# A hybrid encoder layer on one core: the turn of the weights' places in SBUF moved on by one at the end of the first block

## The chip, the core and the metric

The kernel runs on one core of one Trainium2 chip. The metric is the device time of one execution in microseconds (us). Runs of the kernel before took 1068.94 us in the median of three (1068.38 to 1069.08). A profile shows one execution with its five engines: TensorE (PE, with its weight loads as PEld), VectorE (DVE), ScalarE (ACT), GpSimd (POOL) and SyncE (SP, which here only issues transfers).

## The reference

One encoder layer works on 512 tokens of 1024 channels in float32. In the reference's own words, cut to what matters:

```python
x = x + 0.5 * g1 * swiglu(h, w_ffn1_in, w_ffn1_out)          # first feed-forward
h = modulate(rmsnorm(x, norm_mix), sh2, sc2)
qa, ka, va, qb, kb, vb, ga, gb = jnp.split(h @ w_in, SPLIT_POINTS, axis=-1)
ya = window_gqa_sink(rope(qa), rope(ka), va, sink_a) @ w_branch_a
ob = diff_attention(rope(qb), rope(kb), vb, lam)
yb = rmsnorm(ob, subln_b) * (1 - lam_init) @ w_branch_b
x = x + g2 * ((sigmoid(ga) * ya + sigmoid(gb) * yb) @ w_out)  # the mixers
x = x + 0.5 * g3 * swiglu(h3, w_ffn2_in, w_ffn2_out)          # second feed-forward
```

The shifts, scales and gates `sh`, `sc`, `g` come from a product of the conditioning vector with a large matrix `w_mod`. `swiglu` is a product to gate and up halves, `silu(gate) * up`, and a product back. The hidden width is 2816. `ga` and `gb`, 1024 columns each, are the gates of the two mixers: 16 chunks of 128 columns.

## The kernel before

**Three products for one.** Each float32 matrix product is made of three products of numbers in a shorter format. An operand is split in a high part (its value cast) and a low part (what the cast left out), and `mm3` issues high·high, high·low and low·high. So each block of weights is loaded into a `raw` buffer (a ring of four) and split in two: ACT casts the high part, and DVE subtracts to get the low part (`split_from`, L185). For the gates and some projections `load_main` (L1006 to L1014) makes the low part another way: ACT writes the negated high part (L1012), and a transfer issued by POOL adds the weights to it in memory from HBM (L1013).

**The places.** The high parts of all these blocks lie in one tile `high`, the low parts in one tile `low`. Both have five places (`HILO`) of 1024 columns and, at the end, 16 spare columns (`ASIDE`). `high_low` (L192) gives the places out in turn; a counter `turn` modulo five says which is next, and places that a holder still keeps are passed over. A user may lie some columns aside in its place, by `aside` (16 for many; 64 or 56 with blocks of 768 columns in Out1). A block of 1024 columns that lies 16 aside in place i ends 16 columns inside place i+1. In place 4 alone it ends in the spare columns. Whoever shares columns with an earlier user waits for that user's last read, whether he is in the same place or in the one beside it.

**Stages.** The first feed-forward runs in chunks of the hidden width; for each, `Out1` (class at L781) multiplies back. Its last instance (`final`) takes the eight output chunks m in order: m 0 to 3 lie 64 aside, m 4 lies 56 aside, m 5 to 7 lie 16 aside (L802). Then come the boundary to the mixers, `w_vb`, the projections, and the two attentions. In the attention stretch the 16 gate chunks are filler for PE: `gates` (L1106) loads each with `load_main`; gates 3 and 4 are made early, gate 5 (`EARLY_A`) is 16 aside like the projections ahead of it (`project_pairs`, L1083), and gates 6 to 15 are not aside. The branch products `w_yb` and `w_ya` follow. In the second half of `w_ya` the four units lie (16, 16, 0, 0) aside. The output mix has (0, 0, 0, 0, 0, 0, 16, 16), and all of the second feed-forward lies 16 aside.

**What sets the order.** A planner in the kernel writes the main steps and, beside them, small steps with due times. A scheduler then orders the instructions of each engine by what it knows of their dependences, and that includes the columns shared in `high` and `low`. On the chip each engine takes its instructions in that order, and waits at the first that is not ready. The attention steps are scores (L182), exponentials on ACT (L1237), sums and scalings on DVE (L1246 to L1248), transposes on PE (L1150) with a split behind them (L185), products with the values, and a norm with one step on POOL (L1308 to L1314).

The lines of the changed kernel behind L805 have numbers higher by three.

Of the kernel before, what the change touches and what calls it, by code (L numbers as in the profile page):

```python
# [97 lines left out]
RAW, HILO, F2 = 4, 5, 8  # L98
# [36 lines left out]
def layer(ctx: ExitStack, tc: tile.TileContext, a: dict):  # L135
# [48 lines left out]
    def split_from(hi, lo, src):  # L184
        last = S.copy(hi, src), V.tensor_tensor(lo, src, f(hi), ALU.subtract)  # L185
        split[:] = [i.ins for i in last]
# [3 lines left out]
    turn, holders = [0], {}  # L190

    def high_low(n=1024, aside=0, holder=None):  # L192
        while turn[0] % HILO in holders:
            turn[0] += 1
        i = turn[0] % HILO
        turn[0] += 1
        if holder:
            holders[i] = holder
        i = i * 1024 + aside
        return tuple(t[:, i : i + n] for t in parts)  # L200
# [241 lines left out]
    class Unit:  # L442
# [33 lines left out]
        def prepare(self, q):  # L476

            if q in self.ready:
                return
            self.ask(q)  # L480
            n = self.depth * 2 * P
            if q in self.apart:
                both = b8().rearrange("p a b -> p (a b)")
                hi, lo = both[:, 0:n], both[:, 1024 : 1024 + n]
            else:
                hi, lo = high_low(n, ASIDE, (self, q))
            t = self.at[q]
            with tc.issue_after(copied[0]) if q in self.in_order and copied else nullcontext():
                split_from(hi, lo, t)
            self.ready[q] = hi, lo  # L490
            if q in self.more:
                s, src = self.more[q]
                G.dma_start(t, self.srcs[src], accum_op=ALU.add)
                self.at[s] = t
# [286 lines left out]
    class Out1:  # L781
# [17 lines left out]
        def prepare(self, m):  # L799
            if m not in self.ready:  # L800
                self.ask(m)
                aside = FAR if not self.by_halves(m) else STEP_1 if m == NC - LAST_1 else ASIDE  # L802
                t = self.ready[m] = high_low(self.depth * P, aside, (self, m))
                with tc.issue_after(copied[0]):
                    split_from(*t, self.at[m])  # L805
# [1159 lines left out]
```

## Time and profile before

| what | before |
|---|---|
| median of three runs | 1068.94 us (1068.38 to 1069.08) |
| profiled execution, whole | 1068.76 us |
| its span | 1067.0 us |
| mean granted clock of TensorE | 0.995 |
| PE busy | 1047.6 us (98%) |
| DVE busy | 792.1 us (74%) |
| ACT busy | 569.3 us (53%) |
| POOL busy | 154.0 us (14%) |
| moved to and from HBM | 220.53 MB, mean 207 GB/s |

A row of waits names an engine and line, what it waited for, the total in us, how often, and the longest. A row of a timeline names the start, the duration, engine, line, operation, the tile written and the tiles read, their sizes, how many instructions the row joins, and in brackets the idle time before it and what ended it. Matmuls overlap: a row's duration is longer than the distance to the next start. A windows row gives the window, its length, the busy time of each engine with its instructions, the granted clock, the busy share of the transfer engines and GB/s. The chain of work goes back from the last instruction to what released it at each step.

### The profile page before, as it was taken

The page shows a single profiled execution, that of the slowest core. Times are in us where ns is not written, and L with a number is a line of the kernel's source. Part 1 is how long each engine was busy: PE and PEld are TensorE (multiplying, and loading weights), DVE is VectorE, ACT ScalarE, POOL GpSimd, SP SyncE. Part 2 cuts the span into 40 slices and gives each one's busy share as a digit, 9 for nine tenths or more (in the row PEclk, how much of TensorE's full clock was granted, in tenths as well). Part 3 has the DMA queues.
Part 4 walks back from the last instruction along what each step waited for, and adds up shares of the span by engine and source line. Part 5 has one row for each costly group of instructions (what it writes and reads, how often), then busy time and mean ns, then how long its engine had stood idle before and what let it go on. Part 6 is the DMA issues. An engine that isn't in the chain of part 4 may idle for free.

```text
span 1067.0 us, 18682 instructions
## 1 busy us (share of the span) xinstructions
PE 1047.6 (98%) x7330; PEld 957.1 (90%) x7330; DVE 792.1 (74%) x1449; ACT 569.3 (53%) x937; POOL 154.0 (14%) x173
## 2 busy tenths in 40 slices
PE   8999999999999999999899999999999999999998
PEld 5789899899998988899678788989999999999997
DVE  6877667567795779858664577976888787877867
ACT  5645334234354433666666755534766646654553
POOL 1010010100110100452311101001111211112210
PEclk9999999999999999999899999999999999999999
DMA  9888786966885369793647843974498998989974
GB/s 351 306 245 205 212 226 186 271 173 176 251 202 173 119 246 409 216 248 91 168 93 188 226 150 100 364 236 113 102 220 185 221 233 216 221 223 219 207 149 124
DMA packets 69081, 220.53 MB, mean 207 GB/s; under 512 B 8320, under 2 KB 11008, under 8 KB 68992
## 3 DMA queue, kind: packets, MB, share of 16 engines
q1 hardware_dynamic: 46512, 146.52, 38.5%
q0 software_dynamic: 19344, 68.30, 34.4%
q10 hardware_dynamic: 3136, 4.51, 1.2%
q8 instruction: 57, 0.93, 0.3%
q14 instruction: 32, 0.26, 0.1%
HBM read 209.07 MB, written 10.23 MB: 206 GB/s over the span
## 4 chain that ended last, share of the span: by engine, by line
PE 75%; issue 9%; DMA 5%; DVE 5%; ACT 4%; POOL 2%; ACTq 0%; POOLq 0%; DVEq 0%; SPq 0%
PE sc L174 5%; PE sc L176 5%; PE sc L175 5%; PE sc L438 5%; PE sc L440 5%; PE sc L439 4%; PE acc L176 4%; PE acc L174 4%; PE acc L175 4%; PE acc L438 4%; PE acc L440 4%; PE acc L439 4%; PE acc L1072 2%; PE acc L1074 2%; PE acc L1073 2%
## 5 line engine op out<-in xcount | busy, mean ns | idle before, releaser
L185 ACT CAST high<-raw 128x1024 fp32r<-128x1024 f32 (+2 forms) x162 | 158.1, 985 | 158.8 <-PE acc L439 37.3
L185 DVE TENSOR_TENSOR low<-raw,high 128x1024 fp32r<-128x1024 f32 (+2 forms) x162 | 183.7, 1141 | 48.7 <-ACT high L185 47.6
L438 PE MATMUL acc<-b,high 128*128 128x256 f32 x508 | 141.6, 279 | 0.1
L439 PE MATMUL acc<-b,high 128*128 128x256 f32 x508 | 141.3, 278 | 0.1
L440 PE MATMUL acc<-b,low 128*128 128x256 f32 x508 | 141.3, 278 | 0.0
L438 PE MATMUL sc<-b,high 128*128 128x256 f32 x500 | 138.7, 277 | 1.3 <-ACT f L515 1.3
L440 PE MATMUL sc<-b,low 128*128 128x256 f32 x500 | 138.8, 278 | 0.9 <-DVE low L185 0.9
L439 PE MATMUL sc<-b,high 128*128 128x256 f32 x500 | 138.5, 277 | 0.0
L185 DVE TENSOR_TENSOR low<-u,high 128x1024 fp32r<-128x1024 f32 (+1 forms) x73 | 87.5, 1200 | 32.0 <-ACT high L185 30.7
L185 ACT CAST high<-u 128x1024 fp32r<-128x1024 f32 (+1 forms) x73 | 75.5, 1036 | 57.5 <-PE sc L175 15.6
L174 PE MATMUL sc<-b,high 128*128 128x512 f32 (+1 forms) x280 | 100.6, 359 | 0.0
L175 PE MATMUL sc<-b,high 128*128 128x512 f32 (+1 forms) x280 | 100.3, 358 | 0.0
L176 PE MATMUL sc<-b,low 128*128 128x512 f32 (+1 forms) x280 | 100.3, 358 | 0.0
L438 PEld LDWEIGHTS acc<-b,high 128*128 128x128 f32 x508 | 96.0, 189 | 0.6 <-DVE f L517 0.3
L439 PEld LDWEIGHTS acc<-b,high 128*128 128x128 f32 x508 | 96.1, 189 | 0.4 <-DVE b L1754 0.3
L440 PEld LDWEIGHTS acc<-b,low 128*128 128x128 f32 x508 | 96.0, 189 | 0.2 <-DVE low L185 0.2
L438 PEld LDWEIGHTS sc<-b,high 128*128 128x128 f32 x500 | 94.1, 188 | 1.7 <-ACT f L515 1.7
L440 PEld LDWEIGHTS sc<-b,low 128*128 128x128 f32 x500 | 93.9, 188 | 1.4 <-DVE low L185 1.3
L176 PE MATMUL acc<-b,low 128*128 128x512 f32 (+1 forms) x248 | 91.2, 368 | 3.6 <-DMA low<-w_gate 3.6
L439 PEld LDWEIGHTS sc<-b,high 128*128 128x128 f32 x500 | 94.0, 188 | 0.0
L174 PE MATMUL acc<-b,high 128*128 128x512 f32 (+1 forms) x248 | 93.1, 376 | 0.0
L175 PE MATMUL acc<-b,high 128*128 128x512 f32 (+1 forms) x248 | 90.9, 367 | 0.0
(371 smaller groups left out, 2676.6 us busy)
## 6 DMA issues: line engine op xcount, KB each, us to landing
u<-w_mod SPq DMA_DIRECT2D x40, 512.0 KB, 8.4
b<-w_mod SPq DMA_DIRECT2D x32, 512.0 KB, 5.9
raw<-w2i SPq DMA_DIRECT2D x31, 512.0 KB, 5.4
u<-w2i POOLq DMA_DIRECT2D x31, 512.0 KB, 7.3
u<-w1u POOLq DMA_DIRECT2D x24, 512.0 KB, 7.8
raw<-w1u SPq DMA_DIRECT2D x24, 512.0 KB, 6.9
raw<-w1o SPq DMA_DIRECT2D x24, 384.0 KB, 3.9
raw<-w_gate SPq DMA_DIRECT2D x16, 512.0 KB, 5.2
```

The costliest lines, as they stand in the source:

```text
L174: PE.matmul(out, wh, xh, start=first, stop=False)
L175: PE.matmul(out, wh, xl, start=False, stop=False)
L176: PE.matmul(out, wl, xh, start=False, stop=last)
L185: last = S.copy(hi, src), V.tensor_tensor(lo, src, f(hi), ALU.subtract)
L438: PE.matmul(out, wh[:, s], xh, start=first and j == 0, stop=False, skip_group_check=True)
L439: PE.matmul(out, wh[:, s], xl, start=False, stop=False, skip_group_check=True)
L440: PE.matmul(out, wl[:, s], xh, start=False, stop=last and j == 1, skip_group_check=True)
L1072: PE.matmul(out[t][:, 0:n], hh[k][:, ht], wh[:, o : o + n], start=k == 0, stop=False)
L1073: PE.matmul(out[t][:, 0:n], hh[k][:, ht], wl[:, o : o + n], start=False, stop=False)
L1074: PE.matmul(out[t][:, 0:n], hl[k][:, ht], wh[:, o : o + n], start=False, stop=k == NC - 1)
```

## The change

Three lines are added in `Out1.prepare`, ahead of the call of `high_low`. When the last Out1 prepares its first chunk, the counter is moved on until it stands at 1 modulo 5:

```diff
             if m not in self.ready:
                 self.ask(m)
                 aside = FAR if not self.by_halves(m) else STEP_1 if m == NC - LAST_1 else ASIDE
+                if self.final and m == 0:
+                    while turn[0] % HILO != 1:
+                        turn[0] += 1
                 t = self.ready[m] = high_low(self.depth * P, aside, (self, m))
                 with tc.issue_after(copied[0]):
                     split_from(*t, self.at[m])
```

Before, the counter stands at 0 modulo 5 there. So one place is passed over, and that chunk and every user behind it take the next place: what lay in place 0 lies in 1, and so on, and what lay in 4 lies in 0. The distances aside are not changed, and no instruction is added or removed on any engine. The last users of the two kinds meet like this:

| user, aside | place before | place after |
|---|---|---|
| Out1 m 0, 1, 2, 3 (64) | 0, 1, 2, 3 | 1, 2, 3, 4 |
| Out1 m 4 (56) | 4 | 0 |
| `w_kva`, two blocks (16) | 2, 3 | 3, 4 |
| gate 5 (16) | 3 | 4 |
| gate 6 (0) | 4 | 0 |
| gates 7, 8, 9, 10 (0) | 0, 1, 2, 3 | 1, 2, 3, 4 |
| `w_ya`, second half, unit 1 (16) | 3 | 4 |
| `w_ya`, second half, unit 2 (0) | 4 | 0 |
| mix m 0 to 5 (0) | 1, 2, 3, 4, 0, 1 | 2, 3, 4, 0, 1, 2 |
| mix m 6, 7 (16) | 2, 3 | 3, 4 |

## The prediction

> **What bounds the kernel now.** I read the page first, then PE's waits, the chain of work that ended last, and PE's timeline around the longest wait.
>
> ```profile
> span 1067.0 us, 18682 instructions
> ...
> PE 1047.6 (98%) x7330; PEld 957.1 (90%) x7330; DVE 792.1 (74%) x1449; ACT 569.3 (53%) x937; POOL 154.0 (14%) x173
> ```
> ```profile
> PE acc L176 <- DMA low<-w_gate: 3.6, 1, 3.6
> ```
>
> PE is busy for 1047.6 of 1067.0 us. Only 19.4 us are left in which it does nothing, and everything else must show as PE working slowly. The largest single wait is one gate matmul that waits 3.6 us for the transfer that completes a gate's low part. The chain says why that transfer is late:
>
> ```profile
> 520.25 0.95 ACT low L1012
> ...
> 521.49 7.58 DMA low<-w_gate
> ```
> ```profile
> 514.69 1.05 ACT L1011 CAST high<-raw 128x1024 fp32r<-128x1024 f32 x1 [3.69 <-PE acc L175]
> ```
>
> Gate 6's high part is cast only at 514.69, and it is released by a PE matmul of gate 5. Before the change gate 5 lies 16 columns aside in place 3, so its last 16 columns are in place 4, which is gate 6's. The cast therefore waits for gate 5's last use, the low part comes 5.6 us later, its transfer takes 7.58 us, and PE, which comes to it at 525.50, stands until 529.11. Then it runs slowly:
>
> ```profile
> 529.11 0.80 PE L176 MATMUL acc<-b,low 128*128 128x512 f32 x1 [3.61 <-DMA low<-w_gate]
> ...
> 533.55 0.63 PE L174 MATMUL acc<-b,high 128*128 128x512 f32 x1
> 533.98 0.63 PE L175 MATMUL acc<-b,high 128*128 128x512 f32 x1
> ...
> 535.15 0.40 PE L176 MATMUL acc<-b,low 128*128 128x512 f32 x1
> 535.39 0.39 PE L174 MATMUL acc<-b,high 128*128 128x512 f32 x1
> ```
> ```profile
> 169.27:172.68 3.41, 2.47 (x21) 1.00 0.18 47
> 524.26:527.67 3.41, 1.24 (x6) 1.00 0.85 160
> 527.67:531.08 3.41, 1.97 (x5) 0.50 0.37 76
> 531.08:534.50 3.42, 3.42 (x10) 0.50 0.89 204
> 746.12:749.53 3.41, 1.89 (x14) 1.00 0.69 253
> 749.53:752.95 3.42, 3.42 (x18) 0.50 0.48 156
> ```
>
> The second fence is the windows view of PE alone: window, its length, PE busy, granted clock, DMA. From 527.67 to 534.50 the clock is half: matmuls follow each other by 0.43 us (533.55 to 533.98) and not by 0.24 (535.15 to 535.39). All clock changes of the trace lie on a grid of 3.413 us (749.53 is 65 steps after 527.67). After a window with 1.97 us of work or less the next runs at half, after one with 2.47 it does not. The second dip, at 749.53, comes from two waits for lead splits (rival 2).
>
> **The change part by part.** No instruction is added or removed. The turn gains one at the final Out1, so every later user lies one place further, while its distance aside stays. Place 4 is the only one whose aside reaches into the spare columns and into nobody's place. So the price of an aside user followed by one not aside depends on where the pair falls.
>
> *Gate 6's wait, 3.6 us.* Gate 5 now lies in place 4, gate 6 in place 0, and they share no column. In the changed order of instructions gate 6's cast stands on ACT before the `ka` cast of 484.94, and its low part behind it.
>
> ```profile
> 484.94 0.38 ACT L185 CAST ka<-tp 128x256 fp32r<-128x256 f32 x1
> 487.60 0.59 ACT L185 CAST u<-tp 128x512 fp32r<-128x512 f32 x1 [2.28 <-PE tp L1150]
> ```
> ```profile
> 494.56 4.06 POOL L1358 TENSOR_TENSOR rqa<-rqa,half 128x8 f32<-128x8 f32 x2 [14.85 <-DVE rqa L1355]
> ```
> ```profile
> L1009 SPq DMA_DIRECT2D raw<-w_gate x1: 328/328/328, 460.5 to 460.5; - x1
> ...
> DMA to landing us min/median/max: 4.8/4.8/4.8
> ```
>
> ACT is idle for 2.28 us there, and the two parts take 1.05 + 0.95 = 2.0, so ACT is free again at 487.3, before the cast of 487.60. POOL, which issues the low part's transfer, has nothing to do until 494.56. The raw weights are issued at 460.5 and have landed 4.8 us later, at 465.3. Issued at 487.5, and 7.58 long, the low part is complete at about 495, while PE takes up gate 6 at 516.60. The wait of 3.61 goes, with 21 us to spare. If that cover were gone, at most the same 3.61 would come back. The casts that gate 6 leaves behind at 514.69 are taken over by gate 10, which nobody waits for yet.
>
> *The slow clock, 2.5 us.* Without the idle stretch the window from 524.26 is full and the clock stays. From 529.11 to 534.50 PE worked 5.39 us at a pitch of 0.43 in place of about 0.235: 5.39 × (1 − 0.235/0.43) = 2.45. The Trainium skill ("TensorE: Matmul & The Clock Gate", Terms) prices such a stretch as the time at reduced clock times one minus the ratio, 6.83 × 0.5 = 3.4 us; by that sum the time would be 1 us lower. The trace gives 2.45, since 1.44 us of the slow stretch were idle and are counted in the wait already.
>
> *The scores' order, about 2.1 us.* PE's order in this stage changes, because the scheduler has gate 6 as filler from the start.
>
> ```profile
> 517.16 1.89 PE L182 MATMUL sc<-b,b 64*128 64x512 f32 x8
> ...
> 519.17 0.62 PE L182 MATMUL acc<-b,b 64*128 64x512 f32 x2
> ...
> 523.53 0.73 PE L182 MATMUL sc<-b,b 64*128 64x512 f32 x2
> ...
> 524.77 0.73 PE L182 MATMUL sc<-b,b 64*128 64x512 f32 x2
> ...
> 537.30 0.49 PE L182 MATMUL sc<-b,b 64*128 64x512 f32 x1
> 537.30 0.49 PE L182 MATMUL acc<-b,b 64*128 64x512 f32 x1
> ...
> 538.42 0.39 PE L174 MATMUL op<-u,b 128*128 128x256 f32 x1
> ...
> 546.42 0.72 PE L182 MATMUL sc<-b,b 64*128 64x512 f32 x3
> ...
> 549.00 0.66 PE L1150 MATMUL tp<-ident,x 128*128 128x128 f32 x4 [0.93 <-DVE u L185]
> ```
>
> Twelve scores that start two at a time, as both do at 537.30, take about 1.5 us: the dozen at 546.42 is over at about 547.9. The dozen from 517.16 took 2.64, because they went singly as ACT freed their banks, and the next dozen went in three pieces: 0.66 from 523.53 (until transposes at 524.19), 0.73 from 524.77, and 1.12 from 537.30 to 538.42, 2.5 together. Both go in pairs now: 2.6 + 2.5 − 3.0 = 2.1 saved.
>
> *New waits, −2.1 us.* With less on PE between the attention's steps, four groups of transposes come to their operand early.
>
> ```profile
> 548.27 0.68 DVE L185 TENSOR_TENSOR u<-tp,u 128x512 fp32r<-128x512 f32 x1
> ```
>
> Walking the new order by hand with the trace's durations from 516.60, I find: 0.8 at the first group, whose split now stands on DVE behind a scaling of about its own length (bound 0 to 1.4, two such steps); 0.5 for a copy on ACT and 0.5 for a split (each 0 to 0.7, one step); and 1.4 before the transposes that now start at 549.00, where 1.1 are lost today behind the last score (0 to 1.8, today's and one step). Together 3.2, less today's 1.1: 2.1 more, with bounds of −1.1 and +3.5. The sum for this stage is 3.6 + 2.45 + 2.1 − 2.1 = 6.1, between 4.7 and 9.3. Behind 549.00 PE's order is the old one.
>
> *Elsewhere, 0.* In Out1 the changed order has ACT cast chunk 4 before chunks 2 and 3 (rival 4). Place 0 follows place 4 in the second w_ya half: there its third unit is split about 10 us earlier, and its filler goes; PE stood nowhere in this stretch, and by the walk it does not now. In the w_kva stretch one cast moves ahead of two copies that have microseconds to spare. In the second feed-forward every user is aside by 16, the order of instructions is the same, and only the numbers of the places turn.
>
> ```profile
> 640.00:720.00 80.00, 80.00 (x501) 1.00 0.67 232
> ```
>
> The profiled execution took 1068.76, of which 1067.0 are the span and 1.76 lie around it. 1068.76 − 6.1 = 1062.7; the median, 1068.94, stands 0.18 above that execution.
>
> **The rivals.**
>
> *1. ACT becomes the bound of the stage.* It speaks for it that ACT was busy for 23.67 of the stage's 32.40 us:
>
> ```profile
> 516.60:549.00 32.40, 27.82 (x142) 20.48 (x140) 18.56 (x54) 23.67 (x57) 4.77 (x5) 0.89 0.53 123
> ```
>
> In 26.3 us it would be 90% busy, and any step of it out of order stops PE. At the bound of the waits (+3.5), and with the 2.1 of the scores not coming because their banks are freed no sooner, the gain is 3.6 + 2.45 − 3.5 = 2.55: 1066.2. Against it: two casts of gate 6 are gone from it, even if gate 10's replace them.
>
> *2. The second dip goes, or a new one comes.*
>
> ```profile
> 747.88 0.39 PE L438 MATMUL acc<-b,b 128*128 128x256 f32 x1 [0.76 <-ACT b L185]
> ...
> 749.14 0.39 PE L440 MATMUL acc<-b,b 128*128 128x256 f32 x1 [0.76 <-DVE b L185]
> ```
>
> The two lead waits lie at 747.12 to 747.88 and 748.38 to 749.14, both in the window from 746.12. All of this moves 6.1 earlier, which is 2.7 more than one step of the grid. If the grid stands still against the start, the second wait would lie half across a boundary; the window would hold about 2.1 us of work, between 1.97 and 2.47, which the trace leaves open. Without the dip another 3.42 × 0.45 = 1.5 go: 1061.2. In the other direction the new wait of 1.4 plus a neighbour could halve a window: 1064.2. The Trainium skill ("TensorE: Matmul & The Clock Gate", Why this matters for your kernels) allows idle gaps up to about 3 us; by that rule neither two waits of 0.76 nor the new ones can halve the clock. The window from 746.12 contradicts it, so I keep the chance.
>
> *3. It does not do what it says.* The cast could be held by place 0's earlier user or by the ring of raw buffers, and the low part be late again: 1068.8. Against it stand the 21 us to spare.
>
> *4. Slower: Out1's chunk 4 blocks ACT.* Its raw weights are issued late in the stretch:
>
> ```profile
> L794 SPq DMA_DIRECT2D raw<-w1o x1: 328/328/328, 324.4 to 324.4; - x1
> ...
> DMA to landing us min/median/max: 3.2/3.2/3.2
> ```
> ```profile
> 332.71 0.68 DVE L185 TENSOR_TENSOR b<-f,b 128x512 fp32r<-128x512 f32 x1
> ```
> ```profile
> 336.00 0.39 PE L175 MATMUL acc<-b,high 128*128 128x512 f32 x1
> ```
>
> ACT would stand at its cast until 324.4 + 3.2 = 327.6, and behind it wait the casts of chunks 2 and 3, a Silu and the split that DVE ends today at 332.71 + 0.68 = 333.4 and then, by the walk, at about 334.0. PE needs it at 336.0, which leaves 2.0. From a landing of 5.2 us (3.2 + 2.0) PE waits. At 7.58, what gate 6's transfer takes above, it waits 2.4 and, with a slow clock as after 525.50, loses 4.8: 1067.5. At 11 us it waits 5.8 and loses 8.2, which is 2.1 more than the gain: 1070.9, slower by 0.2%, and it goes up with every further microsecond. The 3.2 of this very load speaks against it.
>
> **How the numbers follow.** Forecast: 0.70 for the stage's gain of about 6 with the second dip staying, 1061.7 to 1063.6 (from waits of 0.9 less or 0.9 more than the walk's). Rival 1 0.10, rival 2 0.10 (three quarters of it downward), rival 3 0.05, rival 4 0.05. The range reaches from just below rival 2's 1061.2 past rival 1's 1066.2: 1060.3 to 1066.6. It leaves out rivals 3 and 4 and the low end of the unknown waits. About 0.2% (2.1 us) is what a measurement of this kernel can tell from no change, so faster means below 1066.8: forecast, rivals 1 and 2, 0.90, less 0.03 for a stage that gives back more than its bounds: 0.87. Same 0.07, slower 0.06.
>
> **What would show it.** Right: gate 6's cast at about 485, no wait of PE for `low<-w_gate`, clock 1.00 from 516 to 540, and the transposes of 549.00 at about 543. Wrong: a wait over 2 us between 516 and 545 on ACT or DVE; any PE wait between 320 and 340 or between 670 and 710; half a clock in a window that was full before.

## The result and the profile after

The changed kernel took 1059.51 us in the median of six runs (1058.46 to 1061.06), the kernel before 1067.70 in its six of that comparison (1065.90 to 1069.08): ratio 0.9927, 95% interval 0.9912 to 0.9942. That is 7.8 us faster, with an interval from 6.2 to 9.4. A second comparison on one chip, with more runs (e1 below), gave 0.9942 (0.9928 to 0.9955), 6.2 us. The forecast was 1062.7 with a range from 1060.3 to 1066.6. So the direction held. The forecast gain of 6.1 lies in the middle of the second interval and just outside the first, and the measured time lies 0.8 us below the range.

The page of the profiled execution (1059.46 as a whole, span 1057.7), and PE's waits from 514 to 545 and in all:

```profile
span 1057.7 us, 18680 instructions
...
PE 1042.4 (99%) x7330; PEld 953.6 (90%) x7330; DVE 792.5 (75%) x1449; ACT 567.8 (54%) x937; POOL 153.0 (14%) x173
```
```profile
PE tp L1153 <- DVE u L185: 1.5, 3, 0.8
PE op L1303 <- ACT f L1295: 0.2, 1, 0.2
```

The wait for `low<-w_gate` is gone. PE's busy time fell too, by 5.2 us, though it has the same 7330 matmuls. Of this, 3.6 lie in the stretch of the gates shown below, some 2.45 of them by the clock: at half clock the same matmuls keep PE busy for longer.

What answers to the cast of gate 6 at 514.69, ACT's timeline and POOL's (the numbers of lines are higher by three):

```profile
482.86 1.06 ACT L1014 CAST high<-raw 128x1024 fp32r<-128x1024 f32 x1
483.80 0.39 ACT L185 CAST ka<-tp 128x256 fp32r<-128x256 f32 x1
484.06 1.09 ACT L1015 ACTIVATE low<-raw 128x1024 fp32r<-128x1024 f32 x1
485.54 0.59 ACT L185 CAST u<-tp 128x512 fp32r<-128x512 f32 x1 [0.39 <-PE tp L1153]
```
```profile
485.45 0.91 POOL L1016 DMA_DIRECT2D low<-w_gate  x1 [7.80 <-ACT low L1015]
```

The three lie where the prediction put them, in what was an idle stretch of 2.28; 0.39 of it is left. The cast is 32 us earlier than before. The stretch itself runs from gate 6's first matmul, now at 514.54, to the transposes that were at 549.00. A windows row of it, and PE's timeline:

```profile
514.76:540.41 25.65, 23.98 (x141) 17.84 (x139) 18.76 (x54) 21.49 (x55) 3.95 (x5) 1.00 0.50 118
```
```profile
514.54 0.39 PE L174 MATMUL acc<-b,high 128*128 128x512 f32 x1
...
516.72 0.73 PE L182 MATMUL sc<-b,b 64*128 64x512 f32 x3
...
518.62 0.66 PE L1153 MATMUL tp<-ident,x 128*128 128x128 f32 x4 [0.47 <-DVE u L185]
519.20 0.50 PE L182 MATMUL sc<-b,b 64*128 64x512 f32 x2
519.54 0.39 PE L182 MATMUL acc<-b,b 64*128 64x512 f32 x1
519.87 0.66 PE L1303 MATMUL op<-ident,f 128*128 128x128 f32 x4
...
526.87 0.73 PE L182 MATMUL sc<-b,b 64*128 64x512 f32 x3
...
528.46 0.39 PE L174 MATMUL op<-u,b 128*128 128x256 f32 x1
...
534.32 0.66 PE L1303 MATMUL op<-ident,f 128*128 128x128 f32 x4 [0.19 <-ACT f L1295]
535.20 0.66 PE L1153 MATMUL tp<-ident,x 128*128 128x128 f32 x4 [0.22 <-DVE u L185]
...
540.41 0.66 PE L1153 MATMUL tp<-ident,x 128*128 128x128 f32 x4 [0.79 <-DVE u L185]
```

540.41 − 514.54 = 25.87, where it was 549.00 − 516.60 = 32.40. The stretch is 6.53 us shorter, and the granted clock in it is 1.00 (0.89 before). The four waits stand where the prediction put them: 0.47, 0.19, 0.22 and 0.79.

The rest of the two traces can be compared by the start of each PE instruction in both. Up to 312 us, where PE has the same instructions in the same order, the execution after is already ahead by 2.0 us: PE stands for 0.94 us between 160 and 180 in the one and for 0.09 in the other, and for 0.68 and 0.27 between 240 and 260. At gate 6's first matmul it is 2.06 ahead (516.60 and 514.54), behind the stretch 8.59 (549.00 and 540.41), and so it stays up to 740. At the end of the span it is 9.30 ahead. So 2.8 us of the difference between these two executions lie outside the stretch, most of them ahead of the first place that the change moves.

The second dip of the clock is still there in this execution (windows of PE: window, length, PE busy, granted clock, transfers):

```profile
738.24:741.65 3.41, 1.88 (x14) 1.00 0.72 205
741.65:745.06 3.41, 3.41 (x19) 0.50 0.37 143
```

### The profile page after: what moved, and what is told of

The parts are those of the page before. It is cut to its first block, busy times and chain, and to the rows that moved or that the text cites. A ratio compares the mean times of both kernels' runs of the same rounds, so it can differ in the third digit from the quotient of the medians.

```text
span 1057.7 us, 18680 instructions
## 1 busy us (share of the span) xinstructions
PE 1042.4 (99%) x7330; PEld 953.6 (90%) x7330; DVE 792.5 (75%) x1449; ACT 567.8 (54%) x937; POOL 153.0 (14%) x173
## 4 chain that ended last, share of the span: by engine, by line
PE 74%; issue 9%; DVE 6%; ACT 5%; DMA 4%; POOL 2%; ACTq 0%; POOLq 0%; DVEq 0%; SPq 0%
PE sc L174 5%; PE sc L175 5%; PE sc L176 5%; PE sc L440 5%; PE sc L438 5%; PE sc L439 5%; PE acc L438 4%; PE acc L439 4%; PE acc L440 4%; PE acc L174 4%; PE acc L175 4%; PE acc L176 4%; PE acc L1075 2%; PE acc L1077 2%; PE acc L1076 2%
```

## The experiments

Theory 1: the whole gain is gate 6 no longer sharing columns with gate 5. Theory 2: the places themselves give some 1.5 us more in other stages, since the first comparison gave 7.8 and not 6.1. Each comparison has its own runs of the kernel before on the same chip.

**e1: the changed kernel again**, five rounds.

> The changed kernel once more, beside the kernel before on one chip. Theory 1: the whole gain comes from gate 6 no longer sharing columns with gate 5, 6.5 us in the stretch of PE from 515 to 549 and nothing elsewhere; what the result showed beyond it is spread between executions. Then the ratio is about 0.9939 (6.5 us) and may lie between 0.992 and 0.995. Theory 2: some 1.5 us more come from other stages, by the places themselves. Then the ratio is 0.9925 or less here too, and the profile again is ahead of the one before outside that stretch.

Measured: 1060.54, before 1066.96 (23 runs, 1064.98 to 1070.99), ratio 0.9942 (0.9928 to 0.9955). This is what theory 1 wants. In its profile the stretch of the gates again gives 6.5 us (it runs from 515.10 to 540.96), and the second dip is not there. The two waits that make it are, in PE's timeline of e1:

```profile
739.87 0.39 PE L438 MATMUL acc<-b,b 128*128 128x256 f32 x1 [0.76 <-ACT b L185]
...
741.13 0.39 PE L440 MATMUL acc<-b,b 128*128 128x256 f32 x1 [0.75 <-DVE b L185]
```

They are as long, and as far apart, as in the executions that have the dip (more on this under rival 2 below).

**e2: the turn moved on only at gate 6.**

```diff
+            if j == EARLY_A + 1:
+                turn[0] += 1
             wh, wl = load_main(a["w_gate"][j], ASIDE * (j == EARLY_A))
```

> The kernel before, with the turn moved on by one only when gate 6 takes its place: gate 5 stays in place 3 and gate 6 takes place 0. Everything up to gate 5 keeps its place. Theory 1: gate 6 is split long before PE takes it up, no wait for its low part, the gain of the change returns in full: 6.5 us, ratio 0.994. Theory 2, if the rest comes from the stages ahead of gate 6: about 1.5 us less than the changed kernel, ratio 0.9955 when that has 0.9925.

Measured: 1060.51, ratio 0.9941 (0.9928 to 0.9954): the whole gain, with everything up to gate 5 where it was. So Out1, the boundary and the projections have no part in it that this comparison, about 1.4 us wide to each side, can tell. One wait in the stretch is another, and in all they are as long as those of the changed kernel (PE's waits of e2 from 514 to 550):

```profile
PE tp L1152 <- DVE b L1328: 1.2, 1, 1.2
PE tp L1152 <- DVE u L185: 0.5, 1, 0.5
```

**e3: the change, and one place more at gate 5**, so that 5 and 6 share columns again (the same two lines with `j == EARLY_A`, on the changed kernel).

> The changed kernel, with the turn moved on by one more when gate 5 takes its place: gate 5 lies in place 0 and reaches into place 1, which is gate 6's. All other asides meet as in a kernel two places on. Theory 1: gate 6 is cast only behind gate 5's last use, the wait of about 3.6 us and the slow clock are back, the time is that of the kernel before, ratio 1.000 within 0.002. Theory 2: 1.5 us faster than the kernel before, ratio 0.9985.

Measured: 1068.00, ratio 1.0012 (0.9997 to 1.0026). The wait is back at its old length, on another pair of places (PE's timeline of e3):

```profile
529.58 0.79 PE L176 MATMUL acc<-b,low 128*128 128x512 f32 x1 [3.58 <-DMA low<-w_gate]
```

**e4: the turn moved to 2.**

```diff
-                    while turn[0] % HILO != 1:
+                    while turn[0] % HILO != 2:
```

> The change with 2 in place of 1: all later users lie two places further, gate 5 in place 0 and gate 6 in place 1, with shared columns; PE's order is that of the kernel before throughout. Theory 1: as the kernel before, ratio 1.000 within 0.002. If moving the places as such is worth something (chunk 4 of the last Out1 and the boundary are moved here too): 0.9985 or less.

Measured: 1067.64, ratio 1.0004 (0.9993 to 1.0015). Moving every place is worth nothing that can be told; PE waits for gate 6's low part (3.94 in its profile).

**e5: gate 6's low part made by DVE**, on the kernel before.

```diff
-            wh, wl = load_main(a["w_gate"][j], ASIDE * (j == EARLY_A))
+            if j == EARLY_A + 1:
+                wh, wl = load_split(a["w_gate"][j])
+            else:
+                wh, wl = load_main(a["w_gate"][j], ASIDE * (j == EARLY_A))
```

> The kernel before with its places, so gate 6 still shares columns with gate 5 and is cast behind gate 5's last use at about 514.7. Only gate 6's low part is made by DVE's subtraction from the raw block instead of ACT, POOL and a transfer. If the cost is the late transfer and the slow clock behind it (theory 1): the low part is there at about 517.4, PE waits under 1 us for it, the clock stays at 1.00, and 5 to 6.5 us of gain come without moving any place: ratio 0.994 to 0.9955. If sharing the columns costs by itself, or ACT and DVE bound the stage (rival 1 of the prediction): under 3 us, ratio above 0.997.

Measured: 1062.07, ratio 0.9951 (0.9938 to 0.9965). The columns are still shared and ACT still casts behind gate 5's last matmul, but 1.6 us later DVE begins the low part and PE finds it done. ACT, DVE and PE of e5:

```profile
515.16 1.05 ACT L185 CAST high<-raw 128x1024 fp32r<-128x1024 f32 x1 [3.69 <-PE acc L175]
```
```profile
516.73 1.21 DVE L185 TENSOR_TENSOR low<-raw,high 128x1024 fp32r<-128x1024 f32 x1
```
```profile
517.63 0.50 PE L182 MATMUL sc<-b,b 64*128 64x512 f32 x1
518.06 0.50 PE L176 MATMUL acc<-b,low 128*128 128x512 f32 x1
```

e5's gain of 5.2 us is most of e1's 6.2, and the intervals of the two overlap: sharing columns costs little or nothing by itself here. What costs is what was hung behind it: a cast, a second pass on ACT and a transfer of 7.58 us in a row.

**e6: the changed places only from `w_ya` on** (the turn moved to 4 ahead of the branch's first block).

> The kernel before up to the end of the gates, and the places of the changed kernel from the first block of w_ya on: the branch's third unit of the second half is no longer behind its neighbour, the mix and the second feed-forward lie one place further. Theory 1: 0, ratio 1.000 within 0.0015. If the later stages have a share: 0.9985 or less.

Measured: 1066.29, ratio 0.9991 (0.9978 to 1.0004). Nothing that this comparison can tell. By PE's starts, the mix's steps move about but end within 0.3 us of where they did.

**e8: the turn moved to 4**, which is the kernel before over again.

> The change with 4 in place of 1. Place 4 is still held when the last Out1 prepares its first chunk, so the turn passes over it to place 0, and all places are those of the kernel before: the same instructions in the same order. 1.000, and the width of its interval and the spread of its executions show what any of these comparisons can tell.

Measured: 1066.52 in 12 runs from 1064.56 to 1068.36, ratio 0.9997 (0.9987 to 1.0007). This is the control: single executions of one program lie 4 us apart. Its profile has the wait for gate 6's low part too, but behind it only one window of slow clock, and no second dip:

```profile
523.98:527.39 3.41, 0.00 (x0) 1.00 0.58 114
527.39:530.80 3.41, 3.00 (x7) 0.50 0.60 155
530.80:534.21 3.41, 3.41 (x16) 1.00 0.84 149
```

Here the idle time of 3.85 covers one window wholly and reaches 0.4 into the next, which still holds 3.0 of work; in the profile of before it fell on two windows, 2.17 in one and 1.44 in the next, and both brought a slow window after them. The profiles of e3 and e4, whose waits are 3.58 and 3.94, have two slow windows. That of e6 (3.27), where the window in which the wait begins still holds 2.58 of work, has one.

**e7: no sharing at all.** Places of 1026 columns and asides of 2, on the kernel before.

```diff
-ASIDE = 16
+ASIDE = 2
...
-STEP, STEP_1 = 8, 56
+STEP, STEP_1 = 2, 56
...
-        i = i * 1024 + aside
+        i = i * (1024 + ASIDE) + aside
...
-        parts.append(keep([P, HILO * 1024 + ASIDE], nm, F32R))
+        parts.append(keep([P, HILO * (1024 + ASIDE)], nm, F32R))
```

> The kernel before with its turn, but each place is 1026 columns wide and a user lies 2 aside in place of 16 or 8, so that no user reaches into another's place at all. PE's order in the gate stretch is then that of the changed kernel. Theory 1: the whole gain and no more, ratio 0.994. If sharing costs anywhere else, beyond gate 6: lower than the changed kernel, 0.993 or less.

Measured: 1078.90, ratio 1.0112 (1.0098 to 1.0126), against both theories. By PE's starts the stretch of the gates did gain 6.5 us, but PE lost some 0.2 to 0.4 us in every 10 us of the two feed-forwards. No wait did that; the matmuls follow each other a little more slowly. The mean distance between the starts of neighbouring feed-forward matmuls (128x256) is 118.4 ns, and 114.5 in the kernel before, 114.3 in the changed one. Four more kernels looked for the reason.

**e9: the changed kernel with asides of 2** (the tiles' size kept).

> The changed kernel with asides of 2 columns in place of 16 and 8; places, tile sizes and the order on PE are those of the changed kernel. Theory A (the slow-down without sharing came from where the weights start: columns that are no multiple of 16): the matmuls whose weights start 2 columns aside follow each other by about 117 ns and not 114.5, some 3000 of the two feed-forwards among them, so 6 to 8 us slower than the changed kernel, ratio to the kernel before 0.999 to 1.002. Theory B (it came from the other tiles, which had moved by 24 bytes with the narrower places): as the changed kernel, 0.994.

Measured: 1063.27, ratio 0.9982 (0.9967 to 0.9996), distance 115.5 ns. Between the two theories: weights that start 2 columns aside cost about 1.2 ns a matmul, under a third of the 3.9 that e7 lost.

**e10: no sharing with places of 1032 columns and asides of 8.**

> The kernel before with its turn, places 1032 columns wide and asides of 8, so that nobody reaches into another's place, and all weights start at a multiple of 8 columns. If 8 is enough for the full pace, theory 1 wants the gain of the changed kernel and no more: 0.994. If it is not: between that and the 1.011 of places of 1026. If sharing costs anywhere else: below 0.993.

Measured: 1078.16, ratio 1.0124 (1.0108 to 1.0140), distance 118.2 ns, the same to within a nanosecond for weights at multiples of 16 columns as for those 8 beside.

**e11 and e12: the changed kernel with 16 and 24 unused columns more in each of the two tiles.**

```diff
-        parts.append(keep([P, HILO * 1024 + ASIDE], nm, F32R))
+        parts.append(keep([P, HILO * 1024 + ASIDE + 16], nm, F32R))
```

> The changed kernel with 16 unused columns (64 bytes) more at the end of each of the two tiles of places. Places, asides and the order of every engine are those of the changed kernel; only the tiles laid behind them move by 64 and 128 bytes. If the slower pace of the two kernels without sharing came from where the other tiles then began, and 64 bytes is the grain: as the changed kernel, ratio 0.994, 114.4 ns between the feed-forwards' matmuls.

> The same with 24 unused columns (96 bytes), the size that the two tiles had with places of 1032 columns: all weights start at multiples of 16 columns in their tile, but the second tile begins 96 bytes and the others 192 bytes further. If the moved tiles are the cause: about 118 ns between the matmuls and some 12 us slower than the changed kernel, ratio 1.004 to 1.007. If the places' own columns were the cause: 0.994.

Measured: 1078.06, ratio 1.0105 (1.0088 to 1.0122), and 1084.59, ratio 1.0166 (1.0151 to 1.0182), with distances of 117.8 and 119.9 ns. Both miss what was expected of them, upward. The order of all engines, the places and the asides are those of the changed kernel; only tiles behind the first lie some bytes further. The groups of lines of before, e11 and e12, the same 508 matmuls each:

```profile
L438 PE MATMUL acc<-b,high 128*128 128x256 f32 x508 | 141.6, 279 | 0.1
```
```profile
L438 PE MATMUL acc<-b,high 128*128 128x256 f32 x508 | 143.9, 283 | 0.1
```
```profile
L438 PE MATMUL acc<-b,high 128*128 128x256 f32 x508 | 145.7, 287 | 0.0
```

So where the tiles lie in SBUF changes the pace. That accounts for e10: e12 has the tile sizes of e10 with the places of the changed kernel, and loses no less. It does not account for e7, as the expectation of e9 supposed: in the program built from e7 the two tiles begin at the same addresses as before, and nothing behind them is shifted by the 24 bytes. What changed in e7 is where the weights start inside the tiles, and the pace differs by that start. In its second feed-forward the distance is 116.6, 118.3, 119.9, 118.3 and 118.9 ns for weights in places 0 to 4, which start 2, 4, 6, 8 and 10 columns behind a multiple of 16. Neither is a rule: e9's weights start 2 columns behind as well and follow at 115.5, and in e10 the start makes no such difference. Why the pace goes with these positions stays open. So e7 and e10 say nothing on sharing, and whether it costs anywhere else is open by them; e2, e4 and e6 say that the places of this change have no share in the time but at gate 6 that could be told, to within about 2 us each.

## Why the prediction was right in its mechanism and missed its range

*Gate 6's wait, 3.6 us: right.* It is gone, and the cast, the low part and the transfer lie where they were put. e3 and e4 bring it back by bringing the sharing back, e2 takes it away by that alone. With this rival 3, that the cast would be held all the same, falls.

*The slow clock, 2.45 us: right for the profiled execution, too dear for the kernel.* The stretch's clock is 1.00 now. But 2.45 is what an execution pays whose idle time falls on two windows. The one of e8 ran only 3.00 us of work at half clock, which by the same pitches is 3.00 × 0.45 = 1.35. The other profiles with the wait had 5.70 (e3), 4.95 (e4) and 3.42 us (e6) of it, or 2.6, 2.2 and 1.5. So the term is 1.35 to 2.6 by the execution, with a mean of 2.0 over these five.

*The scores' order, 2.1, and the new waits, −2.1: both too large, and they cancelled.* The waits are 0.47 + 0.19 + 0.22 + 0.79 = 1.67 and not 3.2; less the 0.93 of before that is 0.7 more, where the prediction had 2.1. PE's busy time in the stretch fell from 27.82 to 25.87 − 1.67 = 24.20, by 3.6; 2.45 of that is the clock, so 1.2 is left for the scores, not 2.1. The timeline above agrees: the second dozen does take 1.59 (526.87 to 528.46) and not 2.5, but the first still goes in two pieces, 1.43 from 516.72 to the wait before 518.62 and 0.67 from 519.20, so 2.10 where the prediction had 1.5. A third dozen, from 537.18, is now cut in two and takes 0.2 more than it did. The sum 3.6 + 2.45 + 1.2 − 0.7 = 6.5 is what the stretch shows.

*Elsewhere, 0: right, as far as can be told.* PE's lead is the same at 514 as at 330, and the same at 740 as at 550; in time, e6 for what follows the gates, and e2 beside e1 for what precedes them, leave room for about 2 us each.

*Rival 1, ACT as the bound: no.* ACT is busy for 21.49 of 25.65 us, 84%, and one wait of 0.2 is put down to it.

*Rival 4, Out1's chunk 4: the mechanism is there, the price is not.* ACT did stand for that transfer, but PE was busy throughout (20.00 from 320 to 340, as before):

```profile
325.31 1.57 ACT L185 CAST high<-raw 128x768 fp32r<-128x768 f32 x2 [1.44 <-DMA raw<-w1o]
```

*Rival 2, the second dip: its premise fell.* It supposed the grid of 3.413 us to stand still against the start of the kernel, and asked where the two waits would then lie. From the profile of before to that after the slow window moved from 749.53 to 741.65, by 7.88 us or 2.3 steps, so the grid did not stand still. The profiled executions of before, of the changed kernel and of e5 have the dip; those of e1, e2, e3, e4, e6 and e8 have not, with the same two waits. By PE's starts it is worth 1.5 us each time. It does not belong to the change at all.

Nor does the work in the window decide alone, as the prediction took it. In e1, e4, e6 and e8 the grid parts the two waits or cuts the second, and no window has less than 2.30 us of work. But in e2 both lie in one window, with the same 1.9 us of work as in the profile after, and the next window runs at full clock (windows of e2, counted in steps of 3.413 us from the clock change at 1057.13; e3 is nearly alike with 1.95):

```profile
739.69:743.10 3.41, 1.89 (x15) 1.00 0.76 281
743.10:746.52 3.42, 3.42 (x29) 1.00 0.55 158
```

What else decides stays open. The other direction of this rival, a new slow window by the new waits, did not come.

*The step that failed is "1068.76 − 6.1 = 1062.7" together with the range.* It took one profiled execution for the kernel. That execution had the dear form of the slow clock and the second dip, and its start was slow; the median of the kernel before is 1067.70 in the first comparison, 1.1 us below it, and 1066.96 over 23 runs on the chip of e1, 1.8 us below it, where its runs lie from 1064.98 to 1070.99. The three times shown before, 1068.38 to 1069.08, all lay above that median and close together, and gave no sign of it. The measured 1059.51 is 3.2 us below the forecast: 1.1 are that level, 0.4 are the terms of the stretch (6.5 for 6.1), and 1.7 are left that no run puts down to a stage. As a ratio the prediction was 1062.7/1068.76 = 0.9943, and e1 measured 0.9942. The range was made of the unknown terms of the change alone, with nothing for the spread of executions of one program, which is as wide. The prediction's own bounds for the stage, up to 9.3, reach 1059.5, and the range left that end out; but the waits did not go that way, so a range down to there would have held by luck.

Theory 2 is not borne out: the 1.5 us that the first comparison showed beyond the stretch did not come back in e1 or e2, and no part of the change outside gate 6 was seen to give it. That it is spread between executions is likely and not shown; the pair of traces has an example of such spread in the 2.0 us by which the execution after was ahead before the change begins. Why the starts of two executions differ by that much, up to 312 us, stays open. The waits of PE there that differ most are for a copy on ACT and a split on DVE, and in the chain of before both stand behind transfers (`raw<-w1u`).

## What to carry to other kernels

When one user of a buffer reaches a little into its neighbour, look for the pair whose second user is due soon and has a long chain behind the shared columns; the chain is the price, moving the pair takes it away, and shortening the chain (e5) most of it. Waits of PE that add up to some 1.5 us within 3.4 us can cost more than their length, by a clock that then runs at half for a window, and a wait of 3.6 us cost one such window or two here; whether and how many differs from execution to execution. So a range around a predicted time needs the spread of executions of the unchanged program in it, and a forecast is better made as a difference to the median than to one profile.

## What the runs showed of the hardware that was not expected

- **The clock's grid is free against the kernel.** Two waits of 0.76 us, 1.26 apart, halve the clock for 3.4 us in some executions and not in others. In the profiled executions of before and after, in which they did, a window had 1.89 and 1.88 us of work; in that of e2, in which they did not, one had 1.89 as well. The Trainium skill ("TensorE: Matmul & The Clock Gate", What's actually happening) says that the window of 3413 ns is free-running; the traces agree with that: the dip of before and that of after lie 2.3 windows apart against the start. The Trainium skill's advice to have no idle gaps above about 3 us (same page, Why this matters for your kernels) does not cover the waits of 0.76 that halved the clock in these traces.
- **Where tiles lie in SBUF changes the pace of the matmuls.** With the same instructions in the same order, 64 or 96 unused bytes more per partition in two tiles made the feed-forward matmuls follow each other by 117.8 and 119.9 ns in place of 114.3, and the kernel slower than the changed one by 0.016 and 0.022 of the time of before, 17 and 24 us. Weights that start off a multiple of 16 columns cost about 1.2 ns (e9, 2 columns) and between 2 and 6 ns (e7) of 114. Which of the moved tiles does it, and by what rule, stays open. So a change of a tile's size can cost more than the stall that it removes, and its time says little of anything else until the pace of the matmuls has been looked at.
